# Conditioning loads, merged-row buffers and hidden-row loads moved in a hybrid decoder layer on one core

## The chip, the core and the metric

The kernel runs on one core of a Trainium2 chip. A core has five engines that run their own instruction streams and meet at semaphores: TensorE (PE in the profile; its weight loads are shown as PEld), VectorE (DVE), ScalarE (ACT), GpSimd (POOL) and SyncE (SP), and 16 DMA engines that all of them share. SP only issues transfers here; ACT and POOL issue transfers besides their arithmetic. The transfers of SP and ACT go through hardware queues (q1 and q10 of the profile page), those of POOL through a software queue (q0). The metric is the device time of one execution in microseconds (us).

## The reference

One layer of a decoder trunk is computed for a prompt of 1,024 tokens and for 8 samples of 8 tokens each, with the same weights; the width is 1,024 and the hidden layer of the MLP is 4,096 wide. Cut to what matters (the two branches, a recurrent one and a pooling one, are left out):

```python
def trunk(x, c, shift0, pool0, wkv0, pos0, W):
        ...
        sh, sc, gt = ada_mod(c, lp["w_ada_mix"], lp["b_ada_mix"])
        h = rms_norm(x, lp["norm_mix"]) * (1 + sc) + sh
        P = h @ lp["w_in"]
        ...
        merged = g_r * (o_r @ lp["w_br_rwkv"]) + g_p * (o_p @ lp["w_br_pool"])
        x = x + gt * (merged @ lp["w_out"])
        sh, sc, gt = ada_mod(c, lp["w_ada_mlp"], lp["b_ada_mlp"])
        h = rms_norm(x, lp["norm_mlp"]) * (1 + sc) + sh
        x = x + gt * (jnp.square(jax.nn.relu(h @ lp["w_ff1"])) @ lp["w_ff2"])
        ...
    y = rms_norm(x, W["norm_final"])
```

`ada_mod` multiplies the conditioning vectors c by a 1,024 x 3,072 matrix and gives three thirds: a shift, a scale and the gate `gt`. The gate of the MLP is not needed before the MLP's second product is added to x.

## The kernel before

The activations lie with features on the 128 partitions and tokens along the free axis: 1,088 columns, the 1,024 of the prompt and the 64 of the samples. A "row" below is one block of 128 features by all 1,088 columns, or one half of it (544 columns, 272 KB).

All products are fp32 made of three matmuls at reduced precision: activations and weights are split into a high and a low part, and hi by hi, hi by lo and lo by hi are added up (`mm3`; all matmuls carry line L170). The weights are split as they arrive, by `halves`: ACT copies the high part (`whi`, L193), and DVE or POOL subtracts it for the low part (`wlo`, L194).

The kernel's second half (`phase2`) runs these stages one after another on PE:

- `or_job(m)`, eight jobs that make the merged rows. Each loads two rows from the scratch tensor `d_th` by ACT's queue: `t`, which is the factor of the job's product, and `u`, the addend from the pooling branch. DVE multiplies the product into `t` (L1365), POOL (for the last row, DVE) adds `u` (L1369), then ACT and DVE split the row (L1372, L1373). `t` and `u` come from one ring of four buffers, tag "t".
- `out_job`, the product with `w_out`, and the norm ahead of the MLP.
- `ff1`, the first MLP product, in a form of the Strassen-Winograd scheme: each pair of row blocks j takes seven products c = 0 to 6 in place of eight. Each product is a step of 24 matmuls of 128x272. The scheme's rows of the hidden layer, for each j seven of them, are stored to the scratch tensors `d_ch` and, split already, `d_ch` and `d_cl`. The pairs j = 12 to 15 are kept in another form for a plain product at the end.
- `ada`, the conditioning of the MLP, in three thirds g that run in between on PE. A third takes four steps; each loads two weight tiles of 512 KB by SP into the ring "hid" of four buffers (L290), lets PE do other work for a stated gap, and then runs the tile's matmuls (`wc<-hid`). The third third waits for the hidden rows of j = 11 (`("hid", NE + 3)`), and falls into ff1.
- `ff2`, the second MLP product, in three groups of j (GO = 2, 0, 1). Each group has a phase 0 (c = 0, 1, eight steps), a phase 1 (c = 6, 5, 2, twelve steps) and a phase 2 (c = 4, 3, eight steps). `one_row` loads the rows of the hidden layer that a step needs: for c < 3 and the upper j they are stored as two parts and loaded as such (L1649, L1650); else a row is loaded whole (L1655) and split by ACT (L1656) and DVE (L1657). `tie` ties a split to the end of a step, so that it isn't placed earlier. ACT (L1715) or DVE (L1717) adds up the results of each step.

What sets the order. PE's order is written out: the stages are generators which a pacing rule interleaves by a running sum of matmul times, and the gap of an `ada` step is a number of ns in that sum. The order on DVE, ACT, POOL and SP is set by a scheduler that simulates a timeline when the program is built. On the chip, each engine then runs its own list strictly in that order. A transfer that waits for its buffer holds up everything behind it on the engine that issues it. The transfers of one queue kind also share eight semaphores in turn (`DMAHW0` to `7` for the hardware queues, `DMASW0` to `7` for the software queue), and a transfer waits for the one that had its semaphore before.

Of the kernel before, what the change touches and what calls it, by code (L numbers as in the profile page):

```python
# [9 lines left out]
F32 = mybir.dt.float32  # L10
# [69 lines left out]
class Pace:  # L80
# [24 lines left out]
    def run(self, back, fore=(), until=lambda: False):  # L105
        live = {i: 0.0 for i in range(len(fore))}
        busy = True
        while (live or busy) and not until():
            for i in sorted(live):
                r = live[i]  # L110
                if r() if callable(r) else r <= self.t:
                    try:
                        r = next(fore[i])
                        live[i] = r if callable(r) else self.t + r
                    except StopIteration:
                        del live[i]
                    break
            else:
                r = "idle"
                if busy:  # L120
                    try:
                        r = next(back)
                    except StopIteration:
                        busy = False
                self.dense = r != "idle"
                if r == "idle" and live:
                    self.t += 100
# [9 lines left out]
class K:  # L137
# [1187 lines left out]
    def phase2(self):  # L1325

        nc, io, p = self.nc, self.io, self.p2
        T = lambda: self.row(p, "t", 4)
# [7 lines left out]
        def behind(x):  # L1336

            nc.gpsimd.tensor_copy(x[:, 0:1], self.mark[:, 0:1])
            return x

        def ada():
            yield lambda: ("or", 8) in self.done
            first = 4 * [behind]

            def tile():
                t = self.row(p, "hid", 4)[:, :1024]
                return first.pop()(t) if first else t

            for g in range(3):
                if g == 2:  # L1350

                    self.done.add("ada")
                    yield lambda: ("hid", NE + 3) in self.done
                asb = p.tile([P, 512], F32, tag="wr2", bufs=4, name=self.nm("asb"))
                yield from self.ada_part("w_ada_mlp", g, tile, asb, self.aq, "b_mlp", (8 * g, 8 * g + 4), 5600, 2500, 19000 if g == 0 else 0)

        def or_job(m):
            S = {}

            def begin():  # L1360
                t, S["u"] = T(), T()
                S["t"] = t
                nc.scalar.dma_start(t, self.d_th[m])
                nc.scalar.dma_start(S["u"], self.d_th[8 + m])
                return lambda c0, n, ps: nc.vector.scalar_tensor_tensor(t[:, c0:c0 + n], t[:, c0:c0 + n], 1.0, ps[:, :n], op0=ALU.add, op1=ALU.mult)  # L1365

            def after():
                t = S["t"]
                (nc.vector if m == 7 else nc.gpsimd).tensor_tensor(t, t, S["u"], op=ALU.add)  # L1369
                hi, lo = zip(*[MR() for _ in range(2)])  # L1370
                for i, s in enumerate(split):
                    nc.scalar.activation(hi[i], t[:, s], AF.Copy)  # L1372
                    nc.vector.tensor_tensor(lo[i], t[:, s], hi[i].bitcast(F32), op=ALU.subtract)  # L1373
                mg[0].append(hi)
                mg[1].append(lo)
                self.mark = t
                self.xr.append(HX(F32))
                nc.gpsimd.dma_start(behind(self.xr[m]), io["xT"][m])
                self.done.add(("or", m + 4))

            return Job([io["w_br"][m][:, 0:512]], begin, after=after, xs=lambda: orr, tags=TG)
# [229 lines left out]
        early, steps = [pair_steps(j, 1) for j in range(NE)], []  # L1611
        for j in range(0, NE, 2):
            steps += [early[j][0], early[j + 1][0], early[j][1], early[j + 1][1]]
        for j in [j for k in range(NE) for j in (k, NE + k)]:
            st = pair_steps(j, 2 if j < NE else 0)
            steps += [st[c] for c in ((5, 6, 4, 2, 3) if j < NE else (0, 5, 1, 6, 4, 2, 3))]
        todo = list(steps)
        made = []

        def more():  # L1620
            if todo:
                made.append(todo.pop(0)[0]())
            else:
                self.load2()

        def ff1():
            for _, run, c, j in steps:
                while ("C", c) not in self.done and c > 1:
                    yield "idle"
                yield from run(made.pop(0))  # L1630
                more()
                if j == 15 and c < 2:
                    spread(GO[0], (c,))
                if (j, c) in ((15, 6), (15, 4)):
                    spread(GO[0], (6, 5) if c == 6 else (2,))

        E = {}

        def spread(g, cs, one=1.0):

            for c in cs:
                for k in range(4):
                    one_row(g, c, k, one)

        def one_row(g, c, k, one):
            j = 4 * g + k
            hi, lo = E[c, k] = self.pair(self.hx, "hx", 16) if c < 2 else self.pair(p, "t", 4) if c == 4 else MR()
            if c < 3 and j >= NE:
                nc.sync.dma_start(hi.bitcast(F32), self.d_ch[c][j])  # L1649
                nc.sync.dma_start(lo.bitcast(F32), self.d_cl[c][j])  # L1650
                return
            if k % 2 == 0:
                self.two = self.pair(p, "hid", 4, dt=F32)
            x = self.two[k % 2]
            nc.sync.dma_start(x, self.d_ch[c][j])  # L1655
            nc.scalar.activation(hi, x, AF.Copy, scale=one)  # L1656
            nc.vector.tensor_tensor(lo, x, hi.bitcast(F32), op=ALU.subtract)  # L1657

        def tie(i, x):

            one = g2[:, i % 8, 0:1]
            nc.scalar.activation(one, x[:, 0:1], AF.Copy)
            nc.scalar.activation(one, self.kc("one0")[:, 0:1], AF.Copy)
            return one
# [58 lines left out]
        after = dict(zip(GO, GO[1:]))  # L1723
# [10 lines left out]
        def ff2():  # L1734
            n = 0
            for i, (g, ph, (_, run, c)) in enumerate(sums):
                n = n + 1 if i and sums[i - 1][1] == ph else 0
                yield from run(made.pop(0))
                more()
                one = lambda: tie(i, self.last)  # L1740
                rows = []
                if ph == 0:
                    rows = [(g, c, k) for c in ((2, 4, 3) if g != GO[0] else (4, 3)) for k in range(4)]
                    rows = rows[2 * n:2 * n + 2]
                elif g in after:
                    rows = [(after[g], c, k) for c in ((0, 1) if ph == 1 else (6, 5)) for k in range(4)]
                    rows = rows[n:n + 1] if ph == 2 else rows[n - 2:n - 1] if n > 1 else []
                elif ph == 1 and n in (2, 5):
                    for m in range(n // 3 * 4, n // 3 * 4 + 4):
                        self.xr[m] = HX(F32)  # L1750
                        nc.sync.dma_start(self.xr[m], self.d_xr[m])
                elif ph == 2 and n % 2 == 0:
                    hidden(6, [n // 2], one())
                if rows:
                    apart_now = any(c > 2 or 4 * gr + k < NE for gr, c, k in rows)
                    x = one() if apart_now else 1.0
                    for r in rows:
                        one_row(*r, x)
# [21 lines left out]
        hid = {}  # L1780

        def hidden(grp, rows=range(4), one=1.0):
            for j in rows:
                raw, hi, lo = self.row(p, "hid", 4), self.row(p, "mr", 16, F32R), self.row(p, "mr", 16, F32R)
                nc.sync.dma_start(raw, self.d_hid[4 * (grp - 6) + j])
                nc.scalar.activation(hi, raw, AF.Copy, scale=one)
                nc.vector.tensor_tensor(lo, raw, hi.bitcast(F32), op=ALU.subtract)
                hid[4 * grp + j] = hi, lo
# [22 lines left out]
        def back():  # L1811
            with ExitStack() as c:
                self.psum(c)
                yield from self.stream(None, order, more)
            with ExitStack() as c:
                self.psum(c)
                second, self.load2 = self.stream(None, order2, None, 0)
                yield from ff1()
                yield from ff2()
            self.psum(self.ctx)  # L1820
            self.done.add("sums")
            yield from second
# [142 lines left out]
NE = 8  # L1965
NG = 3
GO = (2, 0, 1)
# [71 lines left out]
```

## Time and profile before

| what | us |
|---|---|
| three runs | 1683.53, 1677.87, 1683.44 |
| median | 1683.44 |
| the profiled execution | 1679.04 |
| its span on the core | 1677.3 |
| PE busy in it | 1608.4 (96%) |
| DVE busy | 1024.6 (61%) |
| ACT busy | 710.8 (42%) |
| POOL busy | 322.0 (19%) |

The mean granted clock of TensorE in the profiled execution is 0.984 of full speed. A row of the timeline gives start and duration in us, engine, line, operation, tile written and tile read; in brackets stands the idle time of the engine before it and what released it. A row of a windows view gives the busy time of each engine in a stretch, with the number of instructions in parentheses, then the granted clock, the share of the DMA engines and GB/s. In the view of waits, a row gives the engine and tile that waited, what it waited for, the total, the number of times and the longest.

### The profile page before, as it was taken

To read this page: it belongs to the slowest core of one execution; us is meant where nothing else is said; L and a number is where in the kernel's file an instruction comes from. 1 tells how busy PE (TensorE), PEld (TensorE's weight loads), DVE (VectorE), ACT (ScalarE), POOL (GpSimd) and SP (SyncE) were. 2 spreads that over 40 slices of the span, in tenths; PEclk is the share of its full clock that TensorE was granted. 3 is DMA by queue.
4 is the path that set the end of the run, shared out by engine and by line. 5 is a ranking of instruction groups with operands and counts; after the bars stand their busy time and mean duration, and the time that the engine had idled before them with its cause. 6 is when DMAs were issued, how large, how long until landed. Compare 5 with 4: busy or idle time off the path is not lost. (4 is left out here: it accounts for less than half of the span.)

```text
span 1677.3 us, 35282 instructions
## 1 busy us (share of the span) xinstructions
PE 1608.4 (96%) x14331; PEld 1495.8 (89%) x14331; DVE 1024.6 (61%) x1723; ACT 710.8 (42%) x1378; POOL 322.0 (19%) x376
## 2 busy tenths in 40 slices
PE   6999999998999999999999999998999999999997
PEld 3989878886888789879989999997999999999997
DVE  5676556735674556334545587775566567675866
ACT  5543343434334333412234374553545556452323
POOL 3311111100000000001621223332223041311221
PEclk9999999999998999999999999998999999999998
DMA  9333414232423142375885465666655956575212
GB/s 335 111 119 128 133 53 137 85 104 77 122 87 114 65 147 78 134 284 185 321 277 178 142 203 184 221 212 214 244 178 188 374 179 216 159 252 180 92 45 107
DMA packets 129474, 279.41 MB, mean 167 GB/s; under 512 B 16768, under 2 KB 31104, under 8 KB 129312
## 3 DMA queue, kind: packets, MB, share of 16 engines
q1 hardware_dynamic: 121632, 255.26, 44.8%
q10 hardware_dynamic: 6048, 16.23, 2.9%
q0 software_dynamic: 1632, 5.67, 1.0%
q8 instruction: 113, 1.85, 0.5%
q14 instruction: 49, 0.40, 0.1%
HBM read 198.15 MB, written 78.95 MB: 165 GB/s over the span
## 5 line engine op out<-in xcount | busy, mean ns | idle before, releaser
L170 PE MATMUL mm<-hx,whi 128*128 128x362 f32 (+1 forms) x1920 | 511.3, 348 | 6.6 <-ACT px L565 2.9
L170 PEld LDWEIGHTS mm<-hx,whi 128*128 128x128 f32 x1920 | 336.8, 192 | 43.2 <-issue 19.2
L170 PE MATMUL pr<-mr,whi 128*128 128x272 f32 x1792 | 337.8, 288 | 2.3 <-ACT whi L193 1.2
L170 PE MATMUL mm<-hx,wlo 128*128 128x362 f32 (+1 forms) x960 | 317.6, 331 | 0.0
L170 PEld LDWEIGHTS pr<-mr,whi 128*128 128x128 f32 x1792 | 281.8, 189 | 5.4 <-ACT whi L193 2.7
L170 PE MATMUL pr<-mr,wlo 128*128 128x272 f32 x896 | 258.5, 288 | 0.8 <-DVE wlo L194 0.8
L193 ACT ACTIVATE whi<-wraw 128x512 fp32r<-128x512 f32 x192 | 120.6, 628 | 240.7 <-PE mm L170 82.8
L170 PEld LDWEIGHTS mm<-hx,wlo 128*128 128x128 f32 x960 | 184.4, 192 | 0.0
L194 DVE TENSOR_TENSOR wlo<-wraw,whi 128x512 fp32r<-128x512 f32 x143 | 110.4, 772 | 110.8 <-ACT whi L193 110.3
L170 PE MATMUL pr<-hx,whi 128*128 128x272 f32 x896 | 169.4, 288 | 3.9 <-DVE hx L1717 1.6
L170 PEld LDWEIGHTS pr<-mr,wlo 128*128 128x128 f32 x896 | 169.2, 189 | 1.0 <-DVE wlo L194 1.0
L170 PE MATMUL mm<-mr,whi 128*128 128x272 f32 (+4 forms) x736 | 154.6, 304 | 2.1 <-DVE t L1365 2.1
L170 PEld LDWEIGHTS pr<-hx,whi 128*128 128x128 f32 x896 | 140.2, 188 | 6.7 <-issue 3.7
L193 ACT ACTIVATE whi<-wr 128x512 fp32r<-128x512 f32 x132 | 82.7, 628 | 142.8 <-PE pr L170 117.6
L170 PE MATMUL pr<-hx,wlo 128*128 128x272 f32 x448 | 128.9, 288 | 0.0
L170 PEld LDWEIGHTS mm<-mr,whi 128*128 128x128 f32 x736 | 120.3, 190 | 9.5 <-issue 5.0
L194 POOL TENSOR_TENSOR wlo<-wraw,whi 128x512 fp32r<-128x512 f32 x49 | 68.3, 1395 | 271.8 <-ACT whi L193 261.5
L170 PE MATMUL mm<-mr,wlo 128*128 128x272 f32 (+4 forms) x368 | 110.8, 301 | 0.0
L170 PE MATMUL pr<-t,whi 128*128 128x272 f32 x448 | 84.4, 287 | 0.0
L170 PEld LDWEIGHTS pr<-hx,wlo 128*128 128x128 f32 x448 | 84.3, 188 | 0.0
L194 DVE TENSOR_TENSOR wlo<-wr,whi 128x512 fp32r<-128x512 f32 x97 | 74.3, 767 | 14.4 <-ACT whi L193 14.4
L194 POOL TENSOR_TENSOR wlo<-wr,whi 128x512 fp32r<-128x512 f32 x35 | 51.1, 1461 | 108.5 <-ACT whi L193 90.9
(396 smaller groups left out, 2646.7 us busy)
## 6 DMA issues: line engine op xcount, KB each, us to landing
wr<-in_w_ff SPq DMA_DIRECT2D x128, 256.0 KB, 3.3
wraw<-in_w_ff SPq DMA_DIRECT2D x80, 256.0 KB, 3.1
hid<-d_ch SPq DMA_DIRECT2D x72, 272.0 KB, 3.9
wraw<-in_w_in SPq DMA_DIRECT2D x68, 256.0 KB, 3.0
d_ch<-hx SPq DMA_DIRECT2D x52, 272.0 KB, 3.5
hid<-in_w_ada_mlp SPq DMA_DIRECT2D x24, 512.0 KB, 5.8
d_th<-px SPq DMA_DIRECT2D x22, 544.0 KB, 3.0
wt<-d_x SPq DMA_DIRECT2D x20, 544.0 KB, 4.3
```

The source lines that it names most:

```text
L170: return self.nc.tensor.matmul(out, lhsT, rhs, **kw)
L193: nc.scalar.activation(hi, raw, AF.Copy)
L194: (nc.gpsimd if pool else nc.vector).tensor_tensor(lo, raw, hi.bitcast(F32), op=ALU.subtract)
```

## The change

Five edits, all in `phase2`:

1. The gap of the conditioning's last third is 18,000 ns of paced time in place of 5,600: its tiles are loaded, and PE does 18 us of other work before it multiplies them.
2. `u` of the merged rows comes from the ring "hid", also of four buffers; the ring "t" then serves `t` alone.
3. The steps of j = 15 run in the order 0, 1, 5, 6, 4, 2, 3 in place of 0, 5, 1, 6, 4, 2, 3.
4. For the first group of ff2, the rows of c = 6, 5 and 2, which were loaded and split during the last steps of ff1, are now loaded and split in its phase 0, two to a step. The rows of c = 4 and 3, before in phase 0, move to phase 1, along with the rows of c = 0 and 1 of the next group, two to a step.
5. All row loads of `one_row`, 96 transfers of 272 KB, are issued by POOL in place of SP. SP's list falls from 796 to 700 rows, POOL's grows by 96.

```diff
-                yield from self.ada_part("w_ada_mlp", g, tile, asb, self.aq, "b_mlp", (8 * g, 8 * g + 4), 5600, 2500, 19000 if g == 0 else 0)
+                yield from self.ada_part("w_ada_mlp", g, tile, asb, self.aq, "b_mlp", (8 * g, 8 * g + 4), 18000 if g == 2 else 5600, 2500, 19000 if g == 0 else 0)
...
-                t, S["u"] = T(), T()
+                t, S["u"] = T(), self.row(p, "hid", 4)
...
-            steps += [st[c] for c in ((5, 6, 4, 2, 3) if j < NE else (0, 5, 1, 6, 4, 2, 3))]
+            steps += [st[c] for c in ((5, 6, 4, 2, 3) if j < NE else (0, 5, 1, 6, 4, 2, 3) if j < 15 else (0, 1, 5, 6, 4, 2, 3))]
...
                 if j == 15 and c < 2:
                     spread(GO[0], (c,))
-                if (j, c) in ((15, 6), (15, 4)):
-                    spread(GO[0], (6, 5) if c == 6 else (2,))
...
             if c < 3 and j >= NE:
-                nc.sync.dma_start(hi.bitcast(F32), self.d_ch[c][j])
-                nc.sync.dma_start(lo.bitcast(F32), self.d_cl[c][j])
+                nc.gpsimd.dma_start(hi.bitcast(F32), self.d_ch[c][j])
+                nc.gpsimd.dma_start(lo.bitcast(F32), self.d_cl[c][j])
                 return
...
-            nc.sync.dma_start(x, self.d_ch[c][j])
+            nc.gpsimd.dma_start(x, self.d_ch[c][j])
...
+                four = lambda g, *cs: [(g, c, k) for c in cs for k in range(4)]
                 if ph == 0:
-                    rows = [(g, c, k) for c in ((2, 4, 3) if g != GO[0] else (4, 3)) for k in range(4)]
-                    rows = rows[2 * n:2 * n + 2]
+                    rows = (four(g, 6, 5, 2) if g == GO[0] else four(g, 2, 4, 3))[2 * n:2 * n + 2]
+                elif ph == 1 and g == GO[0]:
+                    rows = (four(g, 4, 3) + four(after[g], 0, 1))[2 * n:2 * n + 2]
                 elif g in after:
-                    rows = [(after[g], c, k) for c in ((0, 1) if ph == 1 else (6, 5)) for k in range(4)]
-                    rows = rows[n:n + 1] if ph == 2 else rows[n - 2:n - 1] if n > 1 else []
+                    rows = four(after[g], 6, 5)[n:n + 1] if ph == 2 else four(after[g], 0, 1)[n - 2:n - 1] if n > 1 else []
```

Because of the removed lines, lines from L1634 on have numbers lower by one or two in the changed kernel (L1655 becomes L1653, L1656 becomes L1654, L1657 becomes L1655).

How the lists of the engines change is shown at three places. The first is PE in ff1, around the first step of the conditioning's last third (`wc_12984`). Before, it stands directly behind the step that writes `pr_13019`, and the second one (`hid_13048`) follows 30 rows, which are 45 matmuls, further on:

```order
L170 MATMUL pr_13019<-mr_10814,whi_12886 128x272 x2
L170 MATMUL pr_13019<-mr_10814,wlo_12887 128x272
L170 MATMUL wc_12984<-hid_12985,sT 32x512 x2
L170 MATMUL wc_12984<-hid_12987,sT 32x512 x2
L170 MATMUL pr_13061<-mr_11018,whi_12928 128x272 x2
L170 MATMUL pr_13061<-mr_11018,wlo_12929 128x272
```

Now, on PE, `pr_13019` is followed by the next steps of ff1, and the first conditioning step comes 66 rows, which are 99 matmuls, later:

```order
L170 MATMUL pr_13203<-mr_10638,whi_13090 128x272 x2
L170 MATMUL pr_13203<-mr_10638,wlo_13091 128x272
L170 MATMUL wc_12984<-hid_12985,sT 32x512 x2
L170 MATMUL wc_12984<-hid_12987,sT 32x512 x2
L170 MATMUL pr_13203<-mr_10638,whi_13090 128x272 x2
L170 MATMUL pr_13203<-mr_10638,wlo_13091 128x272
```

The following conditioning steps are 141 matmuls apart instead of 45.

The second place is POOL at the end of ff1, before. `wlo_14556` and `wlo_14588` are the low parts of the weights of the last two ff1 steps, (15,2) and (15,3); `L1604` makes a hidden row of j = 7, which SP then stores:

```order
L1512 TENSOR_TENSOR wr_1921_14440<-wr_1921_14440,wr_1911_14360 128x512 [waits DMAHW6_49,DVE_49]
L1604 TENSOR_TENSOR hx_14324<-hx_14391,hx_14324 128x544 [waits DMAHW3_49,DVE_49]
L194 TENSOR_TENSOR wlo_14556<-wr_1921_14440,whi_14555 128x512 [waits PE_49,Activation_49]
L194 TENSOR_TENSOR wlo_14588<-wraw_14585,whi_14587 128x512 [waits DMAHW0_49,PE_49,Activation_49]
L1693 TENSOR_TENSOR wraw_15060<-wr_2019_15028,wraw_15060 128x512 [waits DVE_49,DMAHW1_49,Activation_49,Pool_49]
```

Now 18 row loads stand between L1604 and `wlo_14556` on POOL; the first two (into `hid_14907`, waiting for stores of j = 7) and the eight for c = 0 are followed by these last eight for c = 1:

```order
L1647 DMA hx_14559<-d_ch_8_156 128x544 [waits DMASW4_49,PE_49]
L1648 DMA hx_14559<-d_cl_8_240 128x544 [waits DMASW5_49]
L1647 DMA hx_14562<-d_ch_9_157 128x544 [waits DMASW6_49,PE_49]
L1648 DMA hx_14562<-d_cl_9_241 128x544 [waits DMASW7_49]
L1647 DMA hx_14565<-d_ch_10_158 128x544 [waits DMASW0_49,PE_49]
L1648 DMA hx_14565<-d_cl_10_242 128x544 [waits DMASW1_49]
L1647 DMA hx_14568<-d_ch_11_159 128x544 [waits DMAHW1_49,DMASW2_49,Pool_49]
L1648 DMA hx_14568<-d_cl_11_243 128x544 [waits DMASW3_49]
L194 TENSOR_TENSOR wlo_14556<-wraw_14396,whi_14555 128x512 [waits PE_49,Activation_49]
L194 TENSOR_TENSOR wlo_14600<-wraw_14597,whi_14599 128x512 [waits DMAHW2_49,PE_49,Activation_49]
```

The low parts of the last two steps of ff1 are thus issued behind all these loads; before, the loads were SP's.

The third place is ACT at the turn from phase 0 to phase 1 of the first group. Before, the weights of phase 1's first step, `whi_14996`, stand behind the copies of phase 0's last two results (L1715):

```order
L1715 ACTIVATE hx_14988<-pr_14963 128x544 [waits PE_49]
L1656 ACTIVATE mr_14959<-hid_14955,g_8734 128x544 [waits DMAHW3_49]
L1715 ACTIVATE hx_15025<-pr_15000 128x544 [waits PE_49]
L193 ACTIVATE whi_14996<-wr_2013_14993 128x512 [waits DVE_49]
L193 ACTIVATE whi_15031<-wr_2019_15028 128x512 [waits DVE_49]
```

Now, on ACT, the weights of the first three steps of phase 1 (`whi_14948`, `whi_14989`, `whi_15027`) stand ahead of the last copies (there L1713):

```order
L193 ACTIVATE whi_14948<-wr_1997_14945 128x512 [waits DVE_49,PE_49]
L1713 ACTIVATE hx_14940<-pr_14915 128x544 [waits DMAHW3_49,PE_49]
L193 ACTIVATE whi_14989<-wr_2005_14986 128x512 [waits DVE_49,PE_49]
L1713 ACTIVATE hx_14983<-pr_14958 128x544 [waits PE_49]
L193 ACTIVATE whi_15027<-wraw_15024 128x512 [waits DVE_49,PE_49,Pool_49]
L1713 ACTIVATE hx_14940<-pr_14915 128x544 [waits PE_49]
L193 ACTIVATE whi_15061<-wr_2014_15058 128x512 [waits DVE_49,PE_49]
L1713 ACTIVATE hx_14983<-pr_14958 128x544 [waits PE_49]
```

The weights no longer wait behind the copies of the last two steps of phase 0.

## The prediction

> **What bounds the kernel now.** I read the page's busy times first, then PE's waits, then the timeline and the windows at each wait that the change touches, and last the rows of the engines that would get more to do.
>
> ```profile
> span 1677.3 us, 35282 instructions
> PE 1608.4 (96%) x14331; PEld 1495.8 (89%) x14331; DVE 1024.6 (61%) x1723; ACT 710.8 (42%) x1378; POOL 322.0 (19%) x376
> ```
>
> PE is busy for 96% of the span, and no matmul is taken away. So the change can win only idle time of PE (1677.3 - 1608.4 = 68.9 us in all) and time in which PE ran at a low granted clock; it can lose without limit. PE's waits, longest groups first:
>
> ```profile
> PE mm L170 <- DVE sq L408: 13.9, 2, 12.1
> PE wc L170 <- DMA hid<-in_w_ada_mlp: 7.3, 2, 6.5
> ...
> PE pr L170 <- DVE hx L1717: 2.7, 3, 1.1
> PE mm L170 <- DVE t L1365: 2.1, 1, 2.1
> ...
> PE pr L170 <- ACT whi L193: 1.2, 1, 1.2
> ```
>
> The first is the kernel's start, which no edit touches. The other four lie where the change works: the conditioning's last third (7.3), the merged rows (2.1) and the second product (2.7 + 1.2, and below 0.8 more).
>
> **Part 1, the gap of 18 us.** PE's timeline around the place:
>
> ```profile
> 1152.61 0.29 PE L170 MATMUL pr<-mr,wlo 128*128 128x272 f32 x1
> 1159.41 1.92 PE L170 MATMUL wc<-hid,sT 128*32 128x512 f32 x4 [6.52 <-DMA hid<-in_w_ada_mlp]
> 1162.09 1.92 PE L170 MATMUL wc<-hid,sT 128*32 128x512 f32 x4 [0.76 <-DMA hid<-in_w_ada_mlp]
> ...
> 1171.15 1.07 PE L170 MATMUL wc<-hid,sT 128*32 128x512 f32 x8
> ...
> 1189.55 0.96 PE L170 MATMUL wc<-kct,asb 128*128 128x18 f32 x8
> ```
>
> The windows there:
>
> ```profile
> 1155.00:1158.00 3.00, 0.00 (x0) 0.00 (x0) 2.03 (x4) 0.00 (x0) 0.00 (x0) 0.80 1.02 257
> 1158.00:1161.00 3.00, 1.59 (x4) 0.19 (x4) 0.00 (x0) 0.00 (x0) 0.00 (x0) 0.50 1.04 418
> 1161.00:1164.00 3.00, 2.24 (x7) 0.24 (x5) 0.00 (x0) 0.00 (x0) 0.00 (x0) 0.50 0.70 268
> 1164.00:1167.00 3.00, 3.00 (x15) 3.00 (x14) 0.00 (x0) 0.00 (x0) 0.00 (x0) 0.50 0.55 184
> ```
>
> And the chain that ended last, after it:
>
> ```profile
> 1186.89 2.82 PE pr L170 x21
> ...
> 1190.51 142.06 PE pr L170 x1140
> ```
>
> One ff1 matmul takes 142.06 / 1140 = 0.1246 us at full clock. From the end of the last one before the wait (1152.61 + 0.12 = 1152.73) to 1190.51 pass 37.78 us. In them lie 156 ff1 matmuls (three times the 45 of the order, and 21), 19.4 us; four conditioning steps at the undisturbed 1.07, 4.3 us; and the 0.96. That makes 24.7, so 13.1 us are lost: 7.3 in the two waits, the rest at granted clock 0.50 and in hidden waits further on. The idle time of 6.5 us was followed by a clock of 0.50 that lasted until about 1167. [...]
>
> Is the wait gone? SP issues the tiles as soon as a hidden row of j = 11 is stored:
>
> ```profile
> 1153.64 0.40 SPq L1594 DMA_DIRECT2D d_ch<-hid  x1
> ...
> 1155.74 8.64 SPq L290 DMA_DIRECT2D hid<-in_w_ada_mlp  x4
> ```
>
> That stays. The tiles were there at 1159.41 and 1162.09. With 99 matmuls ahead of it the first step falls at 1152.73 + 99 x 0.1246 = 1165.1, its second half 0.5 later: 5.7 and 3.5 us to spare. The next steps have 141 matmuls, 17.6 us, between them. I take the whole 13.1; the bound on the other side is a tile later by more than 3.5 us, which leaves a remainder of the wait (a rival below).
>
> **Part 2, `u` in the ring "hid".** ACT could issue the load of `t` for m = 7 only when a buffer of the ring of four, shared with `u`, came free. The rows are ACT's queue, DVE, and the windows around it:
>
> ```profile
> 833.65 0.33 ACTq L1363 DMA_DIRECT2D t<-d_th  x1
> ...
> 840.58 0.98 DVE L1365 SCALAR_TENSOR_TENSOR t<-t,mm 128x364 f32<-128x364 f32 x2 [3.45 <-issue]
> ...
> 836.00:839.00 3.00, 3.00 (x25) 2.93 (x24) 1.12 (x2) 0.00 (x0) 1.16 (x1) 1.00 1.03 377
> ...
> 842.00:845.00 3.00, 3.00 (x19) 3.00 (x18) 3.00 (x3) 0.71 (x2) 1.60 (x1) 0.63 0.62 201
> 845.00:848.00 3.00, 3.00 (x24) 2.47 (x23) 2.53 (x4) 1.77 (x3) 1.38 (x4) 0.80 0.46 118
> ```
>
> With four buffers for `t` alone its load goes out four jobs ahead, not two, and the 2.1 us go. Behind them the clock was 0.63 and 0.80: by the clock 3 x 0.37 + 3 x 0.20 = 1.7 us lost, by the matmuls (19 and 24 where 25 is normal) 0.8; I take 1.3, so 3.4 in all, between 2.1 and 3.8. [...] Late next is nothing in this stage: `u` waits only for POOL's additions of four jobs before.
>
> **Parts 3 and 5, row loads on POOL: the block at the end of ff1.** This is the one new wait that I can place. POOL now has 18 row loads ahead of the low parts for (15,2) and (15,3). The rows of before that carry its price (PE's first matmul of (15,0), SP's store of a j = 7 row, POOL's low part, the only POOL loads in the second half, and the first and last of SP's 18 row loads):
>
> ```profile
> 1287.51 0.41 PE L170 MATMUL pr<-hx,whi 128*128 128x272 f32 x2
> ...
> 1288.03 0.33 SPq L1603 DMA_DIRECT2D d_ch<-hid  x1
> ...
> 1297.25 1.29 POOL L194 TENSOR_TENSOR wlo<-wraw,whi 128x512 fp32r<-128x512 f32 x1 [1.07 <-ACT whi L193]
> ...
> L1378 POOL DMA_DIRECT2D hx<-in_xT x8: 552/562/565, 803.6 to 846.5; - x8
> ...
> 1292.59 0.78 SPq L1649 DMA_DIRECT2D hx<-d_ch  x1
> ...
> 1306.20 0.32 SPq L1650 DMA_DIRECT2D hx<-d_cl  x1
> ```
>
> The landing times, from the page and the line of L1378 (minimum, median, maximum):
>
> ```profile
> hid<-d_ch SPq DMA_DIRECT2D x72, 272.0 KB, 3.9
> ...
> d_ch<-hid SPq DMA_DIRECT2D x32, 272.0 KB, 3.4
> hx<-in_xT POOLq DMA_DIRECT2D x8, 544.0 KB, 6.4
> ...
> DMA to landing us min/median/max: 5.1/6.4/7.8
> ```
>
> Everything here comes 13.1 earlier. The block starts when the j = 7 store has landed: 1288.03 - 13.1 + 3.4 = 1278.3. (15,0) starts at 1274.4; five steps of 24 x 0.1246 = 2.99 later, with the order 0, 1, 5, 6, 4, 2, PE reaches (15,2) at 1289.4 and wants its low part at the third matmul, 1289.6. POOL needs 1.29 for it, so the block must be over at 1288.3, after 10.0 us. At POOL's own 0.56 a load it takes 10.1, no stall. At the pace that SP had for the same loads (1306.52 - 1292.59 = 13.9 us) the stall is 3.9. Eight software semaphores allow eight loads in flight, so the last one goes out when two rounds have landed; with the longest landing, 7.8, that is 15.6 + 1.1 = 16.7, a stall of 6.7. I take SP's 13.9, because it is the same data through the same DMA engines. An idle time of 3.9 lies between 2.1, which cost 1.3 of clock, and 6.5, which cost 13.1 - 7.3 - 1.1 = 4.7 (1.1 being the excess of a later conditioning step that waited); linearly 2.7. So +6.6, from 0 to 11.
>
> A like block stands some steps earlier, four loads ahead of the low parts for (6,2): they wait for the conditioning's buffer, at about 1222, take 2.2 at 0.56, and the low part is wanted at 1233. After two other POOL operations and its own 1.29 each there remain about 3 us: nothing, up to 3 if the loads are held up.
>
> **Part 4, the rows of ff2's first group.** PE's waits at the turn to phase 1, the window of phase 0, and DVE's part of a split:
>
> ```profile
> 1333.78 0.52 PE L170 MATMUL pr<-mr,whi 128*128 128x272 f32 x2 [1.23 <-ACT whi L193]
> 1335.06 0.39 PE L170 MATMUL pr<-mr,wlo 128*128 128x272 f32 x1 [0.76 <-DVE wlo L194]
> ...
> 1308.00:1332.00 24.00, 24.00 (x194) 23.98 (x193) 11.56 (x18) 17.37 (x34) 0.00 (x0) 1.00 1.03 386
> ...
> L1657 DVE TENSOR_TENSOR mr<-hid,mr x44: 711/725/1817, 1292.3 to 1505.7; 128x544 fp32r<-128x544 f32 x44
> ```
>
> The 1.2 + 0.8 go, since the weights now stand ahead of the last copies on ACT. Phase 0 gets 12 rows for 8, but four of them are loaded ready. Phase 1 gets 16 split rows in eight steps: 16 x 0.73 = 11.7 us more on DVE in 23.9, beside three or four other operations of about 0.7 a step, which nearly fills it: I take +1.0, between 0 and 2. SP, freed of 96 loads, brings weights earlier: of the 2.7 on L1717 I take -0.5, between 0 and -2.7. Together -1.5, from -4.7 to +1.
>
> **The sum.** -13.1 - 3.4 + 6.6 - 1.5 = -11.4 us against the profiled execution's 1679.0: 1667.6. Two of the three runs lie 4.4 higher, at 1683.5, one and the profiled one near 1678.5, so half of 4.4 is added: 1670.
>
> **The rivals.**
>
> *The block costs nothing* (16 in 100). If the software queue takes a load every 0.56 us and lands them in time, -18.0 is left: 1661.0, with the half of 4.4 1663. For it speaks the row of L1378, against it the 13.9 us on SP.
>
> *The conditioning's wait stays* (7 in 100). The tiles land later than 1165, because their buffers come free later or the DMA engines are full (shares 1.02 and 1.04 above). Then the 13.1 shrink to what 3 us of delay leaves, about 3: 1678, with the half 1680. The 5.7 and 3.5 us to spare speak against it.
>
> *Descriptors held up by DVE* (12 in 100). Where each POOL load waits for one DVE operation (0.73) besides its own 0.56, 18 take 23.2 us, the stall is 13.2 and the clock loses 4.7 more: +17.9 instead of +6.6, 1678.9, with the half 1681. Against it speaks the stretch in which POOL's loads took 552 to 565 ns:
>
> ```profile
> 800.00:850.00 50.00, 47.90 (x298) 46.49 (x297) 28.25 (x45) 14.67 (x25) 34.39 (x32) 0.97 0.85 303
> ```
>
> DVE was busy for 28 of these 50 us. [...]
>
> *Slower: late rows hold up the weights, all through ff2* (15 in 100). ACT's split of a row stands ahead of the next weights' high part. If a pair of rows lands late by the software queue, PE waits in that step. There are 36 such pairs (72 loads). At 1.1 us, the longest wait on L1717 so far, that is +39.6, and 1667.6 + 39.6 = 1707, with the half 1709. It makes the kernel slower by over 0.5% (8.4 us, about what a measurement here can tell from no change) from (11.4 + 8.4) / 36 = 0.55 us a pair. For it speaks a landing of 6.4 against 3.9. Against it: four buffers, each with a pair, let a load go out about three steps, 9.0 us, before its split, and 7.8 was the longest landing.
>
> **How the numbers follow.** The forecast has 50 in 100, all but 2 of it faster. With the free block's 16 that is 64 in 100 for faster by over 0.5% (below 1675). Within 0.5% end the conditioning's wait, the held-up descriptors and those 2: 21. Slower: 15. The low end of the range is the free block with all of ff2's gains, 1661.0 - 3.2 + 2.2 = 1660. The high end takes in the two cases near 1681 with 3 us above them, 1684. The slower rival is left out, with a few in 100 below. The forecast's own range is 1663 to 1676.
>
> **What would show it.** Right: no wait of `wc` on `hid<-in_w_ada_mlp`, and no clock of 0.50 between 1150 and 1170; no wait on L1365; one wait of 3 to 5 us on POOL's `wlo` in the step (15,2), just ahead of phase 0; no wait at the turn to phase 1. Wrong: waits on `wlo` of POOL or on the rows' splits spread over ff2, a `wc` wait at about 1165, or POOL's loads with more than 1 us each.

## The result

| | before | changed |
|---|---|---|
| median of nine runs, us | 1683.08 | 1675.44 |
| lowest and highest | 1677.87, 1688.27 | 1669.14, 1676.57 |
| span of the profiled execution | 1677.3 | 1671.2 |

The ratio of the times is 0.9952, with a 95% interval of 0.9935 to 0.9968: the changed kernel is 5.4 to 10.9 us faster, at the middle 8.1. The prediction had 1670 with a range of 1660 to 1684.

The page of the changed kernel, its first lines:

```profile
span 1671.2 us, 35314 instructions
...
PE 1606.8 (96%) x14331; PEld 1496.4 (90%) x14331; DVE 1029.3 (62%) x1723; ACT 710.3 (43%) x1378; POOL 374.4 (22%) x472
```

POOL is busy for 52.4 us more, which is 96 transfers at 0.54. Of PE's waits in the changed kernel, these are new or larger:

```profile
PE pr L170 <- POOL wlo L194: 5.3, 2, 2.8
...
PE pr L170 <- DVE hx L1715: 3.7, 3, 2.4
...
PE pr L170 <- ACT hx L1534: 2.2, 2, 1.1
```

The groups `wc <- hid<-in_w_ada_mlp` (7.3), `mm <- t L1365` (2.1) and `pr <- whi L193` (1.2) are gone. In place of them stand two waits on POOL's low parts. PE's timeline of the changed kernel at the first steps of the conditioning's last third, at the end of ff1, at the turn to phase 1 (the wait stands in phase 1's third step), in the second group of ff2 and at its end:

```profile
1161.27 1.42 PE L170 MATMUL wc<-hid,sT 128*32 128x512 f32 x8
...
1271.38 0.41 PE L170 MATMUL pr<-hx,whi 128*128 128x272 f32 x2
1275.64 0.52 PE L170 MATMUL pr<-hx,whi 128*128 128x272 f32 x2 [1.10 <-ACT hx L1534]
1290.65 0.39 PE L170 MATMUL pr<-mr,wlo 128*128 128x272 f32 x1 [2.55 <-POOL wlo L194]
1298.02 0.41 PE L170 MATMUL pr<-hx,whi 128*128 128x272 f32 x2
...
1331.05 0.39 PE L170 MATMUL pr<-mr,wlo 128*128 128x272 f32 x1 [2.75 <-POOL wlo L194]
...
1407.56 0.79 PE L170 MATMUL pr<-hx,whi 128*128 128x272 f32 x2 [2.41 <-DVE hx L1715]
...
1559.56 0.50 PE L170 MATMUL mm<-mr,whi 128*128 128x364 f32 x2
```

The same points in the timeline of the kernel before (the first step of ff2, the first matmul behind it):

```profile
1308.42 0.41 PE L170 MATMUL pr<-hx,whi 128*128 128x272 f32 x2
...
1565.61 0.49 PE L170 MATMUL mm<-mr,whi 128*128 128x364 f32 x2
```

With the other starts of stages read in the same way, the lead of the changed kernel grows and shrinks like this:

| point of the program | before | changed | lead | won or lost since |
|---|---|---|---|---|
| first merged rows' product | 835.99 | 834.83 | 1.16 | (no edit ahead of it) |
| first step of ff1 | 951.73 | 947.31 | 4.42 | +3.3 (where edit 2 works) |
| ff1, ahead of the conditioning | 1146.76 | 1142.88 | 3.88 | -0.5 |
| (15,0) | 1287.51 | 1271.38 | 16.13 | +12.2 (where edit 1 works) |
| ff2, phase 0 | 1308.42 | 1298.02 | 10.40 | -5.7 (end of ff1) |
| behind ff2 | 1565.61 | 1559.56 | 6.05 | -4.4 (ff2) |

In this pair of profiles 15.5 us are won early and 10.1 lost late; how much of each row is the work of an edit, the experiments show. Around the conditioning the window of the changed kernel has a busy PE at full clock:

```profile
1150.00:1200.00 50.00, 50.00 (x398) 46.91 (x396) 34.93 (x46) 23.23 (x38) 12.41 (x9) 1.00 0.74 259
```

The block on POOL is there as described; POOL's timeline of the changed kernel:

```profile
1274.38 1.09 POOL L1653 DMA_DIRECT2D hid<-d_ch  x2 [1.48 <-DVE hx L1578]
1275.46 0.54 POOL L1647 DMA_DIRECT2D hx<-d_ch  x1
...
1280.43 0.54 POOL L1647 DMA_DIRECT2D hx<-d_ch  x1 [1.79 <-DMA hid<-d_ch]
...
1288.76 0.54 POOL L1648 DMA_DIRECT2D hx<-d_cl  x1
1289.32 2.51 POOL L194 TENSOR_TENSOR wlo<-wraw,whi 128x512 fp32r<-128x512 f32 x2
```

The first eight loads go out at 0.54 us each. The ninth waits 1.79 us, until the first has landed. From there on ten loads take 8.9 us: their idle times on POOL are 3.6 us for the landing of earlier loads, 1.2 for PE and 0.4 with no releaser in the profile. The 18 loads take 14.9 us, and the low part of (15,2) comes right behind them. PE's clock after the wait, by windows:

```profile
1288.00:1291.00 3.00, 0.45 (x3) 0.36 (x3) 3.00 (x3) 1.71 (x3) 2.75 (x4) 1.00 1.00 382
1291.00:1294.00 3.00, 3.00 (x16) 3.00 (x15) 1.39 (x1) 0.00 (x0) 0.83 (x1) 0.50 0.83 311
1294.00:1297.00 3.00, 3.00 (x24) 3.00 (x24) 0.72 (x1) 0.28 (x1) 0.00 (x0) 0.93 0.61 219
```

16 and 24 matmuls, where the same profile has 26 at full clock (1413 to 1416), are another 1.5 us.

### The profile page after: what moved, and what is told of

The parts are those of the page before. It is cut to its first block, busy times and chain, and to the rows that moved or that the text cites. A ratio compares the mean times of both kernels' runs of the same rounds, so it can differ in the third digit from the quotient of the medians.

```text
span 1671.2 us, 35314 instructions
## 1 busy us (share of the span) xinstructions
PE 1606.8 (96%) x14331; PEld 1496.4 (90%) x14331; DVE 1029.3 (62%) x1723; ACT 710.3 (43%) x1378; POOL 374.4 (22%) x472
## 5 line engine op out<-in xcount | busy, mean ns | idle before, releaser
L193 ACT ACTIVATE whi<-wraw 128x512 fp32r<-128x512 f32 x193 | 121.0, 628 | 254.6 <-PE mm L170 81.5
L194 DVE TENSOR_TENSOR wlo<-wraw,whi 128x512 fp32r<-128x512 f32 x143 | 106.5, 744 | 108.6 <-ACT whi L193 108.1
L193 ACT ACTIVATE whi<-wr 128x512 fp32r<-128x512 f32 x131 | 82.2, 628 | 138.1 <-PE pr L170 97.9
L170 PEld LDWEIGHTS pr<-t,whi 128*128 128x128 f32 x448 | 70.2, 188 | 0.8 <-issue 0.8
```

Of the source, the lines that this page charges most:

```text
L170: return self.nc.tensor.matmul(out, lhsT, rhs, **kw)
L193: nc.scalar.activation(hi, raw, AF.Copy)
L194: (nc.gpsimd if pool else nc.vector).tensor_tensor(lo, raw, hi.bitcast(F32), op=ALU.subtract)
```

## The experiments

The runs ask three things: what the two early edits are worth by themselves, whether the late loss comes from the queue or from the new places of the rows, and by which mechanism. Ratios are to the kernel before, each with its 95% interval; 0.001 is 1.7 us.

| run | ratio | interval |
|---|---|---|
| changed kernel | 0.9952 | 0.9935 to 0.9968 |
| changed kernel again (e12) | 0.9935 | 0.9909 to 0.9961 |
| edit 1 alone (e1) | 0.9909 | 0.9886 to 0.9933 |
| edits 1 and 2 (e2) | 0.9909 | 0.9887 to 0.9930 |
| edit 2 alone (e11) | 0.9985 | 0.9970 to 0.9999 |
| edit 5 alone (e4) | 1.0034 | 1.0018 to 1.0050 |
| edits 1 to 4, loads on SP (e3) | 0.9899 | 0.9878 to 0.9921 |
| all five, two low parts on DVE (e5) | 0.9894 | 0.9868 to 0.9919 |
| all five, 16 loads on SP (e6) | 0.9903 | 0.9876 to 0.9929 |
| all five, the 8 of c = 2 on SP (e7) | 0.9957 | 0.9930 to 0.9984 |
| all five, 24 loads on SP (e8) | 0.9898 | 0.9872 to 0.9924 |
| all five, the 8 of c = 1 on SP (e9) | 0.9917 | 0.9897 to 0.9937 |
| as e5, without edit 3 (e10) | 0.9891 | 0.9874 to 0.9908 |

### The edits apart

Edit 1 alone:

```diff
-                yield from self.ada_part("w_ada_mlp", g, tile, asb, self.aq, "b_mlp", (8 * g, 8 * g + 4), 5600, 2500, 19000 if g == 0 else 0)
+                yield from self.ada_part("w_ada_mlp", g, tile, asb, self.aq, "b_mlp", (8 * g, 8 * g + 4), 18000 if g == 2 else 5600, 2500, 19000 if g == 0 else 0)
```

> Kernel before with the gap of 18 us alone. Both theories: the 12.2 us that the profiles show between the steps around the conditioning's last third (offset -3.9 before it, -16.1 behind it) are the gap's, so about 12 us faster than before, ratio 0.9927. If instead the new places of the row loads had helped the tiles to land earlier, the gap alone gives clearly less, under 8 us.

Edits 1 and 2:

```diff
-                t, S["u"] = T(), T()
+                t, S["u"] = T(), self.row(p, "hid", 4)
```

> Kernel before with the gap and the addends in the ring hid. Theory A (the two early edits carry the whole gain, and edits 3 to 5 cost some 8 us): -12.2 - 3.3 = -15.5 us, ratio 0.9908, faster than the changed kernel by 8. Theory B (edits 3 to 5 cost nothing in net, the late waits come from the earlier arrival at the second product): the same late waits show here too and the ratio is near the changed kernel's 0.9952.

Edit 2 alone:

> Kernel before with the addends in the ring hid alone. By the profile of before 3.3 us faster, ratio 0.998. But the run with the gap alone showed no wait for the merged rows and its median equals that of gap and ring together: if the wait on L1365 is there in some executions only, the ratio is 0.999 to 1.0.

The gap alone is worth 15 us by the times (11 to 19), about the whole lead that the changed kernel had at its best. Theory A holds: with the two early edits only, the kernel is 7 us faster than with all five. Edit 2 is worth little. The run with the gap alone has `t` and `u` in one ring as before, and still PE does not wait for the merged rows. It starts ff1 at 947.88, nearly as early as the changed kernel (947.31), so the 3.3 us of that row are not edit 2's alone. Its windows at the place where the kernel before stood still for 2.1 us:

```profile
836.00:839.00 3.00, 3.00 (x27) 3.00 (x26) 2.32 (x5) 1.69 (x3) 2.01 (x3) 1.00 0.98 397
839.00:842.00 3.00, 3.00 (x27) 3.00 (x26) 2.90 (x3) 0.97 (x3) 1.66 (x2) 1.00 0.75 217
```

And the run with edit 2 alone waits a little there:

```profile
838.21 0.52 PE L170 MATMUL mm<-mr,whi 128*128 128x272 f32 x2 [0.37 <-DVE t L1365]
```

So the wait in the profile of before is not there in each execution of the same code. Edit 2 alone comes out at -2.5 us with an interval from -5.0 to -0.2, and on top of edit 1 nothing is to be seen of it.

### Queue or places

All row loads back on SP, with edits 1 to 4 kept:

```diff
-                nc.gpsimd.dma_start(hi.bitcast(F32), self.d_ch[c][j])
-                nc.gpsimd.dma_start(lo.bitcast(F32), self.d_cl[c][j])
+                nc.sync.dma_start(hi.bitcast(F32), self.d_ch[c][j])
+                nc.sync.dma_start(lo.bitcast(F32), self.d_cl[c][j])
...
-            nc.gpsimd.dma_start(x, self.d_ch[c][j])
+            nc.sync.dma_start(x, self.d_ch[c][j])
```

> Changed kernel with all row loads on SyncE's queue again (edits 1 to 4). Theory A1 (the queue is what costs): no wait on GpSimd's low part at (15,2) nor at the turn to phase 1, 4.5 + 4.0 us gained back, about 1667. Theory A2 (the places of the rows cost, edits 3 and 4): the low-part wait goes, but waits of about the same sum come up elsewhere in the second product, 1673 to 1676.

The reverse of this diff on the kernel before, which is edit 5 alone:

> Kernel before with only the row loads moved to GpSimd's queue. Theory A1: the low parts of (15,2) and (15,3) again stand behind 12 and 18 row loads on GpSimd, a wait of 2 to 5 us there and the clock behind it, 4 to 8 us slower than before, 1687 to 1691. Theory A2: no slower than before, 1683 within 2.

Both speak for the queue. With all loads on SP the kernel gains 17 us in place of 8, and no low part is waited for. Against edits 1 and 2 alone (0.9909) this 0.9899 also says that edits 3 and 4 together bring or cost nothing that the times can show. The queue alone makes the kernel before 5.7 us slower (3.0 to 8.4). PE's waits of that run from 1160 to 1480:

```profile
PE wc L170 <- DMA hid<-in_w_ada_mlp: 10.9, 3, 9.3
PE pr L170 <- ACT hx L1715: 3.9, 1, 3.9
PE pr L170 <- DVE hx L1717: 3.3, 2, 2.5
PE pr L170 <- POOL wlo L194: 1.4, 1, 1.4
```

Without the gap the conditioning's wait is there and longer than the 7.3 of before; that need not be the queue's doing, since the profile of edit 2 alone, with all loads on SP, shows 10.2. The low part and the results of ff2's steps are late. The profiled execution was the slowest of this kernel's twelve (1695.4, with a median of 1689.0), so the sizes here are large ones.

### Order on POOL, or data that is late

The clearest test leaves all 96 loads on POOL, and takes only the two low parts out from behind them:

```diff
                     if c == 2:
...
-                        return self.halves(e, True)
-                    return self.halves(raw("f", 1, 1), True)
+                        return self.halves(e, j < 15)
+                    return self.halves(raw("f", 1, 1), j < 15)
```

> Changed kernel with the low parts of (15,2) and (15,3) made by VectorE; all 96 loads stay where they are on GpSimd. Theory A1a (what costs at the end of the first product is the order on GpSimd, the low part behind 18 loads): the 2.6 us wait and the half clock behind it go, 4.5 us faster than the changed kernel, ratio to before 0.9925; the wait at the turn to phase 1 (2.8 us) stays. Rival A1b (the loads fill the DMA engines and the weights themselves are late): PE waits for the same weights on VectorE or ScalarE instead, ratio 0.995.

The ratio is 0.9894, better than expected. PE's waits of this run from 1230 to 1480, which is the end of ff1 and the first two groups of ff2:

```profile
PE pr L170 <- DVE hx L1715: 4.1, 5, 1.4
PE pr L170 <- ACT hx L1534: 1.1, 1, 1.1
```

Not only the wait at (15,2) is gone, but also the one at the turn to phase 1, which I had expected to stay. The loads are as slow as before (the 18 take 16.6 us, to 1289.30, against 14.9 in the changed kernel), and nobody waits for a low part. So at (15,2) it is the order on POOL that costs, and not data that is late. The timelines of SP suggest why the second wait went with the first. In the changed kernel SP's loads of weights near the block are

```profile
1276.15 0.41 SPq L1674 DMA_DIRECT2D wr<-in_w_ff  x1
...
1286.25 0.33 SPq L1674 DMA_DIRECT2D wr<-in_w_ff  x1
...
1292.42 0.33 SPq L1674 DMA_DIRECT2D wr<-in_w_ff  x1
1292.84 0.98 SPq L1674 DMA_DIRECT2D wraw<-in_w_ff  x2
```

and with the low parts on DVE

```profile
1278.60 3.34 SPq L1674 DMA_DIRECT2D wraw<-in_w_ff  x2
1284.60 3.94 SPq L1674 DMA_DIRECT2D wr<-in_w_ff  x2
```

The two `wraw` loads go into the buffers that the low parts of (15,2) and (15,3) read. In the changed kernel they can't go out before POOL has made these, at 1291.83, and SP's list is in order. The `wr` load just ahead of them waited until 1292.39 for a low part on DVE, which took 3.23 us instead of 0.69 beside POOL's two. In the second profile of the changed kernel (e12, below) DVE's low part took 0.69 and was over before POOL's began, and there SP waits for POOL itself; of its waits between 1270 and 1300:

```profile
SPq L1674 <- POOL wlo L194: 2.0, 2, 1.2
```

With the low parts on DVE the `wraw` loads stand ahead of two `wr` loads in SP's list and go out at 1278.60. Measured from (15,1), which runs at 1273.98 there and at 1275.64 in the changed kernel, that is 12.6 us earlier. How much of it is the buffers and how much SP's other order, which the scheduler made of them, the run doesn't separate. The wait at the turn to phase 1 was for weights that SP had loaded late, as POOL's row there shows in the changed kernel:

```profile
1328.52 1.26 POOL L1691 TENSOR_TENSOR wr<-wraw,wr 128x512 f32<-128x512 f32 x1 [5.69 <-DMA wr<-in_w_ff]
1329.74 1.25 POOL L194 TENSOR_TENSOR wlo<-wraw,whi 128x512 fp32r<-128x512 f32 x1
```

That the block made them late is argued, not shown. The load in question went out at 1321.36, some 29 us behind the block, and the last thing to hold it was a sum on DVE (L1683). In e8, a run below that has no block, POOL's same sum waits no less for its weights:

```profile
1321.66 1.33 POOL L1691 TENSOR_TENSOR wr<-wraw,wr 128x512 f32<-128x512 f32 x1 [6.41 <-DMA wr<-in_w_ff]
```

It starts 29.6 us behind the start of ff2 there, against 30.5 in the changed kernel and 25.4 with the low parts on DVE, and PE does not wait for a low part.

Next, only part of the loads on SP. First the 16 of c = 0 and 1 of the first group:

```diff
-                nc.gpsimd.dma_start(hi.bitcast(F32), self.d_ch[c][j])
+                (nc.sync if c < 2 else nc.gpsimd).dma_start(hi.bitcast(F32), self.d_ch[c][j])
```

(and the same for the low row).

> Changed kernel with the 16 ready rows of c = 0 and 1 of the first group on SyncE, the other 80 on GpSimd. A1a: two loads are left ahead of the low part, the block is gone, 4.5 us faster than the changed kernel, ratio 0.9925, provided that SyncE's weights do not get late behind the 16 loads (A1b: they do, 0.995). The wait at the turn to phase 1 stays in both.

Then with the condition `c == 2`:

> Changed kernel with only the 8 ready rows of c = 2 of the first group on SyncE. They were issued by GpSimd in 1314 to 1322, while the weights of phase 1 came late. If they crowd those weights out because another queue brings them (theory), the wait of 2.8 us at the turn to phase 1 goes with its clock loss, 4.0 us, ratio 0.9928, and the block at (15,2) stays. If the weights are late for another reason (their buffers), the wait stays and the ratio is 0.995.

Then all 24 rows that are stored in two parts (`nc.sync` without a condition):

> Changed kernel with all 24 ready row loads on SyncE and the 72 whole rows on GpSimd. Theory (the two places above are the whole price of the queue): both waits go, 8.5 us faster than the changed kernel, ratio 0.990, the same as with all loads on SyncE. Rival (each load on GpSimd costs something): about a quarter of the 9 us between the changed kernel and the one with all on SyncE, 0.994.

And with the condition `c == 1`, 8 loads:

> Changed kernel with only the 8 ready rows of c = 1 of the first group on SyncE: 10 loads, not 18, stand ahead of the low part of (15,2) on GpSimd. Theory (the block costs by its length beyond the 10 us that are free): the block ends after 8 to 9 us in place of 14.9, PE does not wait for it, and the kernel comes out with the block-free ones, ratio 0.990. Rival (any loads ahead cost in proportion): 10/18 of the 9.8 us stay, ratio 0.993.

Wherever the block in front of (15,2) is short, the ratio is 0.990 to 0.992; with the block in place and the later loads on SP (e7) it stays at 0.9957. My theory for e7, that the loads of c = 2 crowd the weights out, falls: PE's timeline of that run has the block's wait, and then another in place of POOL's,

```profile
1284.66 0.39 PE L170 MATMUL pr<-mr,wlo 128*128 128x272 f32 x1 [2.70 <-POOL wlo L194]
...
1333.83 0.49 PE L170 MATMUL pr<-mr,whi 128*128 128x272 f32 x2 [2.43 <-DVE hx L1715]
```

and SP is held up in the same way (the group of three that begins at 1270.03 takes 16.71 us):

```profile
1270.03 16.71 SPq L1674 DMA_DIRECT2D wr<-in_w_ff  x3
```

e8 leaves 72 loads on POOL and is as fast as e3 with none: a load on POOL costs nothing by itself that the times can show (each interval reaches about 4 us to either side). e9 shows the length that counts. Its timeline of POOL:

```profile
1272.35 1.09 POOL L1653 DMA_DIRECT2D hid<-d_ch  x2 [1.48 <-DVE hx L1578]
...
1280.11 0.54 POOL L1648 DMA_DIRECT2D hx<-d_cl  x1 [0.92 <-PE pr L170]
1280.66 2.55 POOL L194 TENSOR_TENSOR wlo<-wraw,whi 128x512 fp32r<-128x512 f32 x2
```

Ten loads take 8.3 us, and PE does not wait for the low part. Its time can't be told from either expectation (the interval holds both 0.990 and 0.993); the missing wait speaks for the theory. In e6 one wait of 1.1 us on a low part of POOL is left, at 1325.78.

Edit 3, taken out of e5:

```diff
-            steps += [st[c] for c in ((5, 6, 4, 2, 3) if j < NE else (0, 5, 1, 6, 4, 2, 3) if j < 15 else (0, 1, 5, 6, 4, 2, 3))]
+            steps += [st[c] for c in ((5, 6, 4, 2, 3) if j < NE else (0, 5, 1, 6, 4, 2, 3))]
```

> Low parts of (15,2) and (15,3) on VectorE as in e5_low_dve, with the old order 0, 5, 1, 6, 4, 2, 3 of the steps of j = 15. Theory (running c = 1 directly behind c = 0 makes PE wait for ScalarE's copy of the result): the 1.1 us wait ahead of (15,1) goes, 1.1 to 1.3 us faster than e5_low_dve in the profile, below what the times can show. If the order brought something, the wait goes and another comes up by about the same amount.

The wait of 1.1 us on L1534 ahead of (15,1), which is in each profile with edit 3, is gone. Its profiled span is the shortest of all, 1658.9; by the times (0.9891 beside 0.9894) nothing can be told. This and e5, both near 1665 us, are the fastest of the table, but the intervals of e1, e2, e3, e6 and e8 overlap with theirs: edit 1 alone, which changes one number, gives nearly all of it.

The changed kernel once more:

> The changed kernel once more, beside the three above on the same chip: ratio to before 0.995 as before, and the two waits on GpSimd's low parts, at (15,2) and at the turn to phase 1, in its profile; it shows how far two profiles of one kernel differ.

It has both waits again, 3.37 at (15,2) and 1.25 at the turn; a single profile gives such a wait to within about 1.5 us. The timelines of all fourteen profiles tell which stage can be measured by one profile and which can't. The first column goes from PE's first matmul of (15,0) to the first of ff2, the second from there to the first matmul behind ff2:

| kernels | end of ff1, us | ff2, us |
|---|---|---|
| before, e1, e2, e11 | 20.9 in each | 257.2, 259.8, 259.0, 261.8 |
| e10 (no edit 3, low parts on DVE) | 20.9 | 256.1 |
| e4 (edit 5 alone) | 23.0 | 264.3 |
| e3, e5, e6, e8, e9 (edit 3, no long block) | 22.3 in each | 257.3, 257.9, 261.2, 258.8, 259.9 |
| changed, e12, e7 (edit 3 and the block of 18) | 26.6, 28.7, 26.8 | 261.5, 258.3, 262.0 |

At the end of ff1 edit 3 costs 1.4 us, and the block 4.3 to 6.4 more. In ff2 the first four kernels have the same code and lie up to 4.6 us apart, and the two profiles of the changed kernel lie 3.3 apart. So the 4.4 us lost in ff2 by the first pair of profiles are no more than such profiles differ by themselves; e12 loses 1.1.

## Why the prediction was right, and where not

- **Edit 1, -13.1**: right. 12.2 in the profiles, 11 to 19 by the times of e1. The tiles are not waited for, the first matmuls come at 1161.27 and the granted clock from 1150 to 1200 is 1.00. The size came from one execution, in which the waits were 7.3; without the edit they were 10.2 in e11 and 10.9 in e4.
- **Edit 2, -3.4**: over-sized. The two profiles compared show 3.3, but one execution had shown a wait that others don't have, and e1 is as early at ff1 without the edit. Alone it measures -2.5, between -5.0 and -0.2.
- **The block on POOL, +6.6**: the mechanism was right to the row: 18 loads, eight in flight (the ninth waits 1.79 us for the first), 14.9 us where 13.9 was taken, and a wait of 2.55 and 3.37 where 3 to 5 was said. The stage lost 5.7 us in the first profile of the changed kernel and 7.8 in e12. Of this 1.4 is edit 3's, which had been given no price; PE running into ScalarE's copy of the step before (1.10 us on L1534) was overlooked. That wait also brought PE to the low part 1.4 us later: without it, by this sum, the 2.55 would have been 3.9, which is the stall of the forecast. So the total came near the 6.6 although edit 3's wait was missing from the sum, because that wait shortens the block's; this is in part luck.
- **ff2, -1.5**: this step isn't borne out. The wait at the turn on ACT's `whi` went, as said, but one on POOL's `wlo` came in its place two steps later (2.75 and 1.25), for which the step had nothing. "SP, freed of 96 loads, brings weights earlier" was wrong right behind the block: SP's list is in order too, and two of its loads wait for the buffers which the blocked low parts read: these end at 1291.83, and the loads go out at 1292.84. The block was priced only by what stands behind it on POOL, not by who waits for the buffers of what stands behind it. What this costs in ff2 is open: +4.4 in one profile and +1.1 in the other, where kernels with the old ff2 alone differ by 4.6. Of the 4.4, a good part is the wait of 2.41 on L1715 with the slow clock behind it (0.50 for 3.41 us), and the old ff2 has shown one of 2.43 of that kind too (e11, on L1717).
- **The sum**: -11.4 against -6.1 between the two profiles and -8.1 by the times. By the times the two early edits bring 15.3 (e2) where the forecast had 16.5, and edits 3 to 5 cost 7.2 (changed kernel against e2) where it had 5.1. Both lie within their intervals, so the times don't say which term was off. The whole price of the block is 7 to 10 us by the times (0.9935 and 0.9952 against e5's 0.9894, each with an interval of several us); 4.3 to 6.4 of it is seen directly at the end of ff1.
- **The rivals**: the free block and the conditioning's wait did not come. Descriptors held up by DVE did not show: POOL's 18 loads took 0.54 us each in a stretch of 14.9 us in which DVE was busy for 4.7, and the idle times between them were for the most part for landings (3.6 us of 5.2). Late rows all through ff2 did not show either, since e8 with 72 loads on POOL is as fast as e3.

## What to carry to other kernels

A transfer that is moved to an engine that also computes must be read in that engine's order: what stands behind it, how long the queue lets the transfers wait for each other (here the ninth load 1.79 us for the first), and whose buffers the delayed instructions hold. Work that is needed at a fixed time goes ahead of a long run of loads, or on another engine; here two subtractions moved to another engine brought the ratio from 0.9935 and 0.9952 to 0.9894. A wait of 2 us that one execution shows should be looked for in a second one before it goes into a sum at full size, and so should a loss of a few us that two profiles show over a long stage.

## What was not expected of the hardware

Idle times of two to three us did not always cost clock. After 2.55 us (changed kernel), 2.70 (e7) and 2.41 (changed kernel, 1407) the granted clock was 0.50 to 0.51 for the next 3 us, after 3.37 (e12) for 6 us; after 2.43 (e7) it stayed at 1.00, as the windows show (the 2.70 first, then the 2.43):

```profile
1285.00:1288.00 3.00, 3.00 (x16) 3.00 (x15) 1.39 (x1) 0.00 (x0) 0.83 (x1) 0.51 0.81 287
...
1331.00:1334.00 3.00, 0.57 (x5) 0.38 (x4) 3.00 (x6) 2.35 (x7) 0.40 (x1) 1.00 0.25 87
1334.00:1337.00 3.00, 3.00 (x25) 3.00 (x25) 3.00 (x4) 2.08 (x4) 2.52 (x4) 1.00 0.72 192
```

Where the half clock lies at the 2.41 of the changed kernel, two rows of its windows show:

```profile
1403.64:1407.05 3.41, 1.51 (x13) 1.29 (x11) 2.07 (x4) 1.66 (x3) 1.07 (x2) 1.00 0.99 336
1407.05:1410.46 3.41, 2.90 (x13) 2.93 (x14) 3.41 (x6) 2.79 (x8) 1.92 (x3) 0.50 0.75 238
```

PE is idle for 1.90 us of the first row, at a clock of 1.00; the second row, in which the wait ends, is at 0.50 over its 3.41 us. In the same profile the clock was 0.50 from 1291.00 to 1294.41, behind the 2.55, and from 1331.96 to 1335.37, behind the 2.75, as long each time: by the clock 1.7 us lost in each. The length of a wait alone thus doesn't tell what it costs, which the forecast's linear estimate took it to do. Why the 2.41 cost clock and the 2.43 of e7 did not is not shown.
